# A two-layer trunk on one core: the feed-forward network in units of 1024 columns, half of its k-tiles as seven block products

## The chip, the core and the metric

The kernel runs on one core of a Trainium2 chip. The time is device time of one execution in microseconds (us), as a median of several. In the core, TensorE (PE) multiplies; its weight loads are counted apart (PEld). VectorE (DVE) and ScalarE (ACT) compute on tiles of 128 partitions, GpSimd (POOL) does little here, and SyncE (SP) issues the DMA transfers. Matmuls write to PSUM, everything else lives in SBUF.

## What is computed

Two layers over 256 tokens of width 2048, in fp32. Each has an input projection to 7168 columns, a gated and an attention branch, an output projection, and a feed-forward network (FFN) of width 5632:

```python
for l in range(DEPTH):                      # 2
    z = rms_norm(x, mix_norm[l]) @ w_in[l]  # 2048 x 7168
    mixed = ...                             # gated half and dilated attention, each normed
    x = x + mixed @ w_out[l]
    h = rms_norm(x, ffn_norm[l])
    x = x + (silu(h @ w_gate[l]) * (h @ w_up[l])) @ w_down[l]
```

w_gate and w_up are 2048 x 5632, w_down 5632 x 2048.

## The kernel before

Every fp32 product is made of three matmuls: an operand is split into a high and a low part (fp32r), and high x high, high x low and low x high are added in PSUM (L787 to L789). A matmul takes 128 rows of k, 128 tokens and 512 columns. A `Block` is 256 tokens x 512 columns: for each k-tile of 128 rows six matmuls, three for each token tile, into two PSUM banks `Z0`, `Z1`. A k-tile's six matmuls take 1.36 us.

Weights stream through a ring. `dma_to` (L685) fetches two k-tiles (`KC = 2`, 512 KB) into `raw`, five buffers. `split_to` has ACT copy them to `wh` (rounded to fp32r) and DVE compute `wl = raw - wh`, both 128x1024; four buffers each, three pairs ahead of the matmuls. All ACT, DVE and POOL instructions go through one helper, so they carry line L86.

An FFN layer is eleven times a gate block and an up block (16 k-tiles each) and then four down blocks of 44 k-tiles. After a gate block ACT makes `s = silu(Z * r2)`; after an up block DVE multiplies `s` by `Z * r2`, PE transposes it (8 transposes into `hTp`, L246), ACT and DVE split the result into `hTh` and `hTl`. A down block is added to the residual `xs` at its end. This side work is written as generators ("jobs"); rough clocks of the queues decide at build time, after every k-tile, which step is issued next. The order on each engine is then fixed, and each engine goes through its list in order.

Of the kernel before, what the change touches and what calls it, by code (L numbers as in the profile page):

```python
# [103 lines left out]
class Lease:  # L104
    """A count of buffers; each comes back at a time of the queue clocks."""
# [17 lines left out]
class Block:  # L123
    """One [256 tokens, 512 columns] output block: a list of k-tiles streamed through PSUM."""

    def __init__(self, src, kts, operand, done):
        self.src = src
        self.kts = kts
        self.operand = operand
        self.done = done  # L130
# [3 lines left out]
def trunk_kernel(ctx: ExitStack, tc: tile.TileContext, aps: dict):  # L134
# [6 lines left out]
    t2_lease = Lease(q, 5)  # L141
# [137 lines left out]
    for l, L in enumerate(layers):  # L279
# [26 lines left out]
    # ------------------------------------------------------------ layer consts  # L306
    def layer_consts(L):
# [30 lines left out]
    # ---------------------------------------------------------------- mixer  # L338
    def qk_done(L, pair, first):
        """Two kinds (k and q of group 0, or q of groups 1 and 2) of two heads each: RMS norm per  # L340
        head, rotary, transposition to [head dim, token]."""
        def job(Z):
# [11 lines left out]
            yield from t2_lease.take(4)  # L354
# [538 lines left out]
```

## Time and profile before

| | |
|---|---|
| median of 3 runs | 2343.61 us (2343.33 to 2343.93) |
| the profiled execution: span | 2342.1 us |
| PE busy | 2334.6 us (100%) |
| DVE busy | 1299.6 us (55%) |
| ACT busy | 1120.8 us (48%) |
| DMA moved | 440.23 MB, mean 188 GB/s |

The profile is of one execution; its span goes from the first to the last instruction, and the median of the runs is 1.5 us above it. Matmul rows overlap each other: a row's length is not the time from one to the next.

### The profile page before, as it was taken

How to read it: one execution, taken by the hardware profiler on the slowest of the kernel's cores; microseconds unless marked ns; L12 is line 12 of the kernel's file. 1: busy time of each engine (PE TensorE's matmuls, PEld its weight loads, DVE VectorE, ACT ScalarE, POOL GpSimd, SP SyncE). 2: the span in 40 equal slices, each digit the busy share in tenths (PEclk: the TensorE clock that was granted, in tenths of full speed). 3: DMA queues.
4: the chain of work that ended last, by engine and by line, in shares of the span. 5: the costliest groups of instructions: out<-in, count | busy, mean ns of one | idle time of the engine just before them, and what ended most of it. 6: DMA issues, size and time to landing. Idle time of an engine off the chain costs nothing.

```text
span 2342.1 us, 27917 instructions
## 1 busy us (share of the span) xinstructions
PE 2334.6 (100%) x10633; PEld 1937.0 (83%) x10633; DVE 1299.6 (55%) x1587; ACT 1120.8 (48%) x1548; POOL 43.3 (2%) x36
## 2 busy tenths in 40 slices
PE   9999999999999999999999999999999999999999
PEld 7888888888888888888888888888888888888887
DVE  6676676645445445444465667765454454454443
ACT  6556565544444444444455565655444444443333
POOL 0000000000000000000000000000000000000000
PEclk9999999999999999999999999999999999999999
DMA  8655555666565566556665555556666565556664
GB/s 301 208 173 169 173 160 180 189 190 190 187 193 192 185 193 190 189 190 192 192 195 194 175 164 178 162 180 183 195 187 190 189 188 190 190 193 194 201 201 135
DMA packets 122822, 440.23 MB, mean 188 GB/s; under 512 B 14272, under 2 KB 14784, under 8 KB 122432
## 3 DMA queue, kind: packets, MB, share of 16 engines
q1 hardware_dynamic: 122688, 438.45, 59.1%
q8 instruction: 83, 1.36, 0.2%
q14 instruction: 51, 0.42, 0.0%
HBM read 436.30 MB, written 2.10 MB: 187 GB/s over the span
## 4 chain that ended last, share of the span: by engine, by line
PE 99%; DMA 0%; DVE 0%; SPq 0%; ACT 0%; issue 0%
PE Z L789 32%; PE Z L787 32%; PE Z L788 32%; PE sc L448 1%; PE hTp L246 1%; PE qkp L246 1%; PE o L480 0%; PE xTp L246 0%; PE gt L543 0%; DMA raw<-in_w_in 0%; PE pT L471 0%; PE aTp L246 0%; PE bTp L246 0%; DVE xs L86 0%; DVE wl L86 0%; ACT wh L86 0%
## 5 line engine op out<-in xcount | busy, mean ns | idle before, releaser
L86 DVE TENSOR_TENSOR wl<-raw,wh 128x1024 fp32r<-128x1024 f32 (+1 forms) x817 | 999.3, 1224 | 992.3 <-ACT wh L86 991.7
L86 ACT ACTIVATE wh<-raw 128x1024 fp32r<-128x1024 f32 (+1 forms) x817 | 864.1, 1059 | 1082.8 <-PE Z L789 1040.6
L787 PE MATMUL Z<-wh,xTh 128*128 128x512 f32 x2304 | 911.0, 395 | 1.5 <-ACT wh L86 1.5
L789 PE MATMUL Z<-wh,xTl 128*128 128x512 f32 x2304 | 898.2, 390 | 0.0
L788 PE MATMUL Z<-wl,xTh 128*128 128x512 f32 x2304 | 897.1, 389 | 0.8 <-DVE wl L86 0.8
L789 PEld LDWEIGHTS Z<-wh,xTl 128*128 128x128 f32 x2304 | 432.4, 188 | 91.6 <-DVE xTl L86 0.2
L787 PEld LDWEIGHTS Z<-wh,xTh 128*128 128x128 f32 x2304 | 432.9, 188 | 89.5 <-ACT wh L86 2.8
L788 PEld LDWEIGHTS Z<-wl,xTh 128*128 128x128 f32 x2304 | 433.1, 188 | 87.9 <-DVE wl L86 1.5
L787 PE MATMUL Z<-wh,hTh 128*128 128x512 f32 x704 | 274.4, 390 | 0.0
L789 PE MATMUL Z<-wh,hTl 128*128 128x512 f32 x704 | 274.0, 389 | 0.0
L788 PE MATMUL Z<-wl,hTh 128*128 128x512 f32 x704 | 273.9, 389 | 0.0
L789 PEld LDWEIGHTS Z<-wh,hTl 128*128 128x128 f32 x704 | 132.1, 188 | 27.6
L787 PEld LDWEIGHTS Z<-wh,hTh 128*128 128x128 f32 x704 | 132.2, 188 | 27.3
L788 PEld LDWEIGHTS Z<-wl,hTh 128*128 128x128 f32 x704 | 132.2, 188 | 27.2
L86 ACT ACTIVATE p<-s,m 128x384 f32<-128x384 f32 (+1 forms) x32 | 24.9, 777 | 56.3 <-DVE m L86 56.2
L787 PE MATMUL Z<-wh,bTh 128*128 128x512 f32 x128 | 50.7, 396 | 0.0
L787 PE MATMUL Z<-wh,aTh 128*128 128x512 f32 x128 | 50.0, 391 | 0.0
L789 PE MATMUL Z<-wh,bTl 128*128 128x512 f32 x128 | 49.9, 390 | 0.0
L789 PE MATMUL Z<-wh,aTl 128*128 128x512 f32 x128 | 49.9, 389 | 0.0
L788 PE MATMUL Z<-wl,bTh 128*128 128x512 f32 x128 | 49.8, 389 | 0.0
L788 PE MATMUL Z<-wl,aTh 128*128 128x512 f32 x128 | 49.8, 389 | 0.0
L86 ACT ACTIVATE junk<-Z,r 128x128 bf16<-128x128 f32 x128 | 46.5, 363 | 5.5 <-POOL r L86 2.4
(98 smaller groups left out, 1014.4 us busy)
## 6 DMA issues: line engine op xcount, KB each, us to landing
raw<-in_w_in SPq DMA_DIRECT2D x223, 512.0 KB, 3.5
raw<-in_w_gate SPq DMA_DIRECT2D x176, 512.0 KB, 3.5
raw<-in_w_up SPq DMA_DIRECT2D x176, 512.0 KB, 3.5
raw<-in_w_down SPq DMA_DIRECT2D x176, 512.0 KB, 3.4
raw<-in_w_out SPq DMA_DIRECT2D x64, 512.0 KB, 3.5
xstage<-in_xT SPq DMA_DIRECT2D x8, 256.0 KB, 7.2
xs<-in_x SPq DMA_DIRECT2D x2, 1024.0 KB, 9.2
out<-xs SPq DMA_DIRECT2D x8, 256.0 KB, 2.2
```

What stands on the lines that cost most here:

```text
L86: return f(**kw)
L246: nc.tensor.transpose(out=tp[:, i, t * P:(t + 1) * P], in_=src_of(t)[:, (c0 + i) * P:(c0 + i + 1) * P], identity=ident)
L448: nc.tensor.matmul(out=sc[:, g, :n], lhsT=L.kv[pair, g][:, h, t * P:(t + 1) * P], rhs=kT[:, h, :n], start=True, stop=True)
L787: nc.tensor.matmul(out=Z[t], lhsT=hi, rhs=wh[:, k, :], start=n == 0, stop=False)
L788: nc.tensor.matmul(out=Z[t], lhsT=hi, rhs=wl[:, k, :], start=False, stop=False)
L789: nc.tensor.matmul(out=Z[t], lhsT=lo, rhs=wh[:, k, :], start=False, stop=n == len(b.kts) - 1)
```

## The change

In the FFN a unit is now 256 tokens x 1024 columns: the gate and the up block of one column tile, or two neighbouring down blocks. Of its k-tiles, eight (columns 0 and 1 of the operand, four k-tiles each) are treated as a 2 x 2 block product: the operand's blocks are (token tile) x (k half), the weights' (k half) x (column half). Seven products take the place of eight (Winograd's form of Strassen's method). The other k-tiles stay plain, in items of four k-tiles and one column half (24 matmuls).

The seven products r1, r5, r6, r2, r7, r3, r4 need seven weights: three blocks as they are, and e = b22 - b12, b12 - b11, e + b11 and b21 less that, four DVE sums of 128x2048. Each is then split as before, now in 128x2048 pieces (names p1 to p7 in the code, in the same order). They also need seven operands (`FORMS`), made by `make_forms` with four DVE sums and seven splits of 128x512. Sums of products are formed in four PSUM banks C1, CX, CY, CZ: after r1 ACT copies C1 to CX, after r5 CZ to `s5`, after r6 CX to CY, after r7 CX to `s3`; DVE then adds s3 to CZ and s5 to CY. Then come the plain items: gate 2, up 2, gate 3, up 3 (gate columns in C1 and CX, up columns in CY and CZ). Up 2 starts only when both sums are made.

The down product is taken in three chunks of k (`CHUNKS`): after four gate/up units two down units over their 16 k-tiles, the same again, and after the last three two down units whose treated pair is only two k-tiles wide (products of 6 matmuls). After each down unit DVE adds the four banks to `xs`.

Buffers are now one pool `gen` of 22 slots of 8 KB, for operands, raw weights, splits and tables alike; weights may hold five raw slots and six split slots in the FFN. The input and output projections stay blocks of 512 columns, with transfers of four k-tiles (1 MB). The four PSUM banks are leased one by one.

On PE 384 of 9792 main matmuls go.

DVE in the middle of a gate/up unit of layer 0. `wl` is a low half, `s` the gated product, `hTl` or `hF` low parts of h. Before:

```order
L86 TENSOR_TENSOR wl_5730<-raw_5661,wh_5729 128x1024
L86 TENSOR_TENSOR wl_5748<-raw_5679,wh_5747 128x1024
L86 TENSOR_TENSOR wl_5768<-raw_5697,wh_5767 128x1024
L86 SCALAR_TENSOR_TENSOR s_5635<-Z0_5615,r20_3967,s_5635 128x512
L86 SCALAR_TENSOR_TENSOR s_5636<-Z1_5616,r20_3967,s_5636 128x512
L86 TENSOR_TENSOR wl_5788<-raw_5715,wh_5787 128x1024
L86 TENSOR_TENSOR wl_5818<-raw_5733,wh_5817 128x1024
L86 TENSOR_TENSOR hTl_5806<-hTp_5807,hTh_5805 128x512
L86 TENSOR_TENSOR wl_5838<-raw_5751,wh_5837 128x1024
L86 TENSOR_TENSOR hTl_5806<-hTp_5812,hTh_5805 128x512
L86 TENSOR_TENSOR wl_5858<-raw_5771,wh_5857 128x1024
L86 TENSOR_TENSOR wl_5876<-raw_5791,wh_5875 128x1024
```

After, in the unit that also makes the forms of a chunk:

```order
L90 TENSOR_TENSOR wl_4110<-raw_3967,wh_4109 128x2048
L90 TENSOR_TENSOR raw_3909<-raw_3967,raw_3909 128x2048
L90 TENSOR_TENSOR wl_4133<-e_3998,wh_4132 128x2048
L90 TENSOR_TENSOR wl_4153<-raw_3949,wh_4152 128x2048
L90 TENSOR_TENSOR wl_4181<-raw_3909,wh_4180 128x2048
L90 TENSOR_TENSOR wl_4201<-raw_4060,wh_4200 128x2048
L90 TENSOR_TENSOR CZ_4116<-CZ_4116,s3_4130 128x512
L90 TENSOR_TENSOR wl_4221<-raw_4114,wh_4220 128x2048
L90 TENSOR_TENSOR hF_4232<-xg_3891,hF_4232 128x512
L90 TENSOR_TENSOR wl_4244<-raw_4136,wh_4243 128x2048
L90 TENSOR_TENSOR CY_4150<-CY_4150,s5_4129 128x512
L90 TENSOR_TENSOR hF_4232<-xg_3891,hF_4232 128x512
```

Before there is one kind of piece, 128x1024, with small work between; now 128x2048 pieces, a sum of weights (`raw` or `e` as the output) between them, and the sums into CZ and CY behind several of them.

ACT around the silu of a gate block. Before:

```order
L86 ACTIVATE wh_5579<-raw_5507 128x1024
L86 ACTIVATE wh_5597<-raw_5527 128x1024
L86 ACTIVATE wh_5617<-raw_5547 128x1024
L86 ACTIVATE s_5635<-Z0_5451,r20_3967 128x512
L86 ACTIVATE s_5636<-Z1_5452,r20_3967 128x512
L86 ACTIVATE wh_5639<-raw_5565 128x1024
L86 ACTIVATE wh_5657<-raw_5583 128x1024
L86 ACTIVATE wh_5675<-raw_5601 128x1024
L86 ACTIVATE wh_5693<-raw_5621 128x1024
```

After, from the end of the unit that makes the forms to the first copy of the next unit:

```order
L90 ACTIVATE wh_4309<-raw_4184 128x2048
L90 ACTIVATE wh_4338<-raw_4204 128x2048
L90 ACTIVATE hF_4233<-xg_3891 128x512
L90 ACTIVATE wh_4370<-raw_4184 128x2048
L90 ACTIVATE hF_4233<-xg_3891 128x512
L90 ACTIVATE hF_4234<-xg_3891 128x512 x2
L90 ACTIVATE fF_3286<-xg_3891 128x512
L90 ACTIVATE s_4384<-C1_4093,r20_3748 128x512
L90 ACTIVATE s_4386<-CX_4107,r20_3748 128x512
L90 ACTIVATE CX_4403<-C1_4390 128x512
```

The silu of C1 stood directly behind weight halves; it now stands behind the high parts of five forms.

DVE where the FFN of layer 0 begins: the low parts of the last four columns of the normed x (`xTl`, now `fT`). Before:

```order
L86 TENSOR_TENSOR wl_3892<-raw_3819,wh_3891 128x1024
L86 TENSOR_TENSOR wl_3924<-raw_3837,wh_3923 128x1024
L86 SCALAR_TENSOR_TENSOR xTl_3912<-xTp_3913,ffng_88,xTh_3911 128x256 x2
L86 TENSOR_TENSOR wl_3946<-raw_3855,wh_3945 128x1024
L86 SCALAR_TENSOR_TENSOR xTl_3912<-xTp_3918,ffng_88,xTh_3911 128x256 x2
L86 TENSOR_REDUCE rs_3968<-fss0_95 128x2
L86 TENSOR_SCALAR rsq_3970<-rs_3968 128x2
L86 TENSOR_TENSOR wl_3974<-raw_3875,wh_3973 128x1024
L86 TENSOR_TENSOR wl_3992<-raw_3895,wh_3991 128x1024
L86 TENSOR_TENSOR wl_4010<-raw_3927,wh_4009 128x1024
L86 TENSOR_TENSOR wl_4028<-raw_3949,wh_4027 128x1024
```

After, inside the first gate/up unit:

```order
L90 TENSOR_TENSOR wl_3661<-raw_3570,wh_3660 128x2048
L90 TENSOR_TENSOR CY_3584<-CY_3584,s5_3563 128x512
L90 SCALAR_TENSOR_TENSOR fT_3686<-fTp_3687,ffng_81,fT_3686 128x256 x2
L90 TENSOR_TENSOR wl_3709<-raw_3590,wh_3708 128x2048
L90 TENSOR_TENSOR e_3712<-raw_3646,raw_3627 128x2048
L90 TENSOR_TENSOR raw_3627<-raw_3627,raw_3608 128x2048
L90 TENSOR_TENSOR wl_3740<-raw_3608,wh_3739 128x2048
L90 TENSOR_TENSOR raw_3608<-e_3712,raw_3608 128x2048
L90 SCALAR_TENSOR_TENSOR fT_3686<-fTp_3692,ffng_81,fT_3686 128x256 x2
L90 TENSOR_REDUCE rs_3749<-fss0_88 128x2
L90 TENSOR_SCALAR rsq_3751<-rs_3749 128x2
```

Between the two pairs of low parts stood one piece of 128x1024; now two splits and three sums of 128x2048 stand there, among them those of the next unit.

The core of the diff; lines that are only "..." mark what is left out:

```diff
@@ -30,15 +30,19 @@
 NQ = len(DIL)
 EPS = 1e-6
 BIG = 1e30
-KC = 2
-
-RAW_BUFS = 5
-W_BUFS = 4
-SPLIT_AHEAD = 3
-DMA_AHEAD = SPLIT_AHEAD + RAW_BUFS - 1
-GEN_BUFS = 30
-
-MM_NS = 214
+KC = 4
+HK = 2
+S_GU = 4
+FORMS = ("11", "22", "S1", "S3", "S2", "12", "S4")
+
+SLOTS = 22
+PLAIN_RAW, PLAIN_RING = 3, 4
+UNIT_RAW, UNIT_RING = 5, 6
+CHUNKS = ((4, 4), (4, 4), (3, 2))
+
...
-    t2_lease = Lease(q, 5)
+    t2_lease = Lease(q, 2)
+    rot_lease = Lease(q, 1)
     sd_lease = Lease(q, 2)
     sc_lease = Lease(q, 1)
     unit_lease = Lease(q, UNITS)
...
-    raw_p = ctx.enter_context(tc.tile_pool(name="raw_p", bufs=RAW_BUFS))
-    w_p = ctx.enter_context(tc.tile_pool(name="w_p", bufs=W_BUFS))
-    tmp = ctx.enter_context(tc.tile_pool(name="tmp", bufs=5))
+    gen = ctx.enter_context(tc.tile_pool(name="gen", bufs=SLOTS))
...
+    def make_forms(F, xg):
+
+        def quarter(t, h):
+            return xg[:, h, :F.s, t * P:(t + 1) * P]
+        a11, a12, a21, a22 = quarter(0, 0), quarter(0, 1), quarter(1, 0), quarter(1, 1)
+
+        def split(f, src):
+            hi, lo = F.at(f)
+            act.activation(out=hi, in_=src, func=ACTF.Copy)
+            dve.tensor_tensor(out=lo, in0=src, in1=hi.bitcast(F32), op=ALU.subtract)
+            F.ready.add(f)
+        split("11", a11)
+        yield
+        split("22", a22)
+        yield
+        dve.tensor_tensor(out=a22, in0=a21, in1=a22, op=ALU.add)
+        dve.tensor_tensor(out=a21, in0=a11, in1=a21, op=ALU.subtract)
+        yield
+        split("S1", a22)
+        yield
+        dve.tensor_tensor(out=a11, in0=a22, in1=a11, op=ALU.subtract)
+        split("S3", a21)
+        yield
+        split("12", a12)
+        yield
+        split("S2", a11)
+        yield
+        dve.tensor_tensor(out=a12, in0=a12, in1=a11, op=ALU.subtract)
+        split("S4", a12)
+
+
...
+    class Chunk:
+
+
+        def __init__(self, L, j0, n, s):
+            self.L, self.j0, self.n, self.s = L, j0, n, s
+            self.table, self.F, self.xg = {}, None, None
+
+        def put_h(self, j, src_of):
...
+                self.F = F
+                yield from make_forms(F, self.xg)
+
...
+    def gu_bank(L, j, chunk):
+
+        s = {}
+
+        def done(n, t, bank):
+            if n == 0:
+                yield lambda: hasattr(L, "r2")
+                yield from t2_lease.take(1)
+                s[t] = t2("s")
+                act.activation(out=s[t], in_=bank, func=ACTF.Silu, scale=L.r2[:, t:t + 1])
+                mm_lease.give()
+                return
+            yield lambda: t in s
+            dve.scalar_tensor_tensor(
+                out=s[t], in0=bank, scalar=L.r2[:, t:t + 1], in1=s[t], op0=ALU.mult, op1=ALU.mult)
             mm_lease.give()
-            L.s[j] = s
-        return job
...
+    def dma_one(r):
+        n = sum(src.shape[1] for src in r.srcs)
+        r.tile = slot([P, n, W], F32, "raw")
+        k = 0
+        for src in r.srcs:
+            nc.sync.dma_start(out=r.tile[:, k:k + src.shape[1], :], in_=src)
+            k += src.shape[1]
+        live[0] += 1
...
+    def w_sum(out, in0, in1, op):
+        saved, q.chain = q.chain, q.pe
+        dve.tensor_tensor(out=out, in0=in0, in1=in1, op=op)
+        q.chain = saved
+
+    def mm3(out, x, wh, wl, start, stop):
+        hi, lo = x
+        for n, (a, b) in enumerate(((hi, wh), (hi, wl), (lo, wh))):
+            nc.tensor.matmul(
+                out=out, lhsT=a, rhs=b, start=start and n == 0, stop=stop and n == 2,
+                skip_group_check=True)
...
+    def unit(s, quarter, plains, form, done):
+
+
+
+        bank = {}
+        b11, b12, b22, b21 = (Raw([quarter(*kn)], UNIT_RAW) for kn in ((0, 0), (0, 1), (1, 1), (1, 0)))
+        raws.extend((b11, b12, b22, b21))
+        U = {}
+
+        def new_bank(name):
+            drain(lambda: mm_lease.free)
+            mm_lease.free.pop(0)
+            bank[name] = mm_p.tile([P, W], F32, tag="mm", name="C" + name)
+
+        def copy(out, in_):
+            saved, q.chain = q.chain, q.pe
+            act.activation(out=out, in_=in_, func=ACTF.Copy)
+            q.chain = saved
+
+        def early():
+            x11, x12, x22 = need(b11), need(b12), need(b22)
+            U["e"] = slot([P, s, W], F32, "e")
+            live[0] += 1
+            w_sum(U["e"], x22, x12, ALU.subtract)
+            w_sum(x12, x12, x11, ALU.subtract)
+
+        def p1(it, parts=1):
+            it.w = split_w(b11.tile)
+            w_sum(b11.tile, U["e"], b11.tile, ALU.add)
+
+        def p5(it, parts=1):
+            it.w = split_w(b12.tile)
+            live[0] -= 1
+
+        def p6(it, parts=1):
+            it.w = split_w(b11.tile)
+
+        def p2(it, parts=1):
+            it.w = split_w(need(b21))
+            w_sum(b11.tile, b21.tile, b11.tile, ALU.subtract)
+            live[0] -= 1
+
+        def p7(it, parts=1):
+            it.w = split_w(U["e"])
+            live[0] -= 1
+
+        def p3(it, parts=1):
+            it.w = split_w(b22.tile)
+            live[0] -= 1
+
+        def p4(it, parts=1):
+            it.w = split_w(b11.tile)
+            live[0] -= 1
+
+        def product(it, f, name, start):
+            wh, wl = it.w
+            for k in range(s):
+                x = form(f, k)
+                mm3(bank[name], x, wh[:, k, :], wl[:, k, :], start and k == 0, k == s - 1)
+                q.pe += 3 * MM_NS
+                run_jobs()
+
+        def r1(it):
+            new_bank("1")
+            product(it, "11", "1", True)
+            new_bank("X")
+            copy(bank["X"], bank["1"])
+
+        def r5(it):
+            new_bank("Z")
+            product(it, "S1", "Z", True)
+            U["s5"], U["s3"] = (tmp.tile([P, W], F32, tag="u", name=n) for n in ("s5", "s3"))
+            copy(U["s5"], bank["Z"])
+
+        def r6(it):
+            product(it, "S2", "X", False)
+            new_bank("Y")
+            copy(bank["Y"], bank["X"])
+
+        def r2(it):
+            product(it, "12", "1", False)
+
+        def r7(it):
+            product(it, "S3", "X", False)
+            copy(U["s3"], bank["X"])
+
+            def sums():
+                dve.tensor_tensor(out=bank["Z"], in0=bank["Z"], in1=U["s3"], op=ALU.add)
+                yield lambda: "p3" in U
+                yield from pause(0)
+                dve.tensor_tensor(out=bank["Y"], in0=bank["Y"], in1=U["s5"], op=ALU.add)
+                U["summed"] = True
+            add(sums(), FFN_LIMIT)
+
+        def r3(it):
+            product(it, "S4", "Y", False)
+            U["p3"] = True
+
+        def r4(it):
+            product(it, "22", "X", False)
+
+        for p, r in ((p1, r1), (p5, r5), (p6, r6), (p2, r2), (p7, r7), (p3, r3), (p4, r4)):
+            items.append(Item(1 if s <= 2 else 2, UNIT_RING, p, r))
+        items[-7].early = early
+
+        names = {(0, 0): "1", (1, 0): "Y", (0, 1): "X", (1, 1): "Z"}
+        for i, (n, srcs, ops) in enumerate(plains):
+            r = Raw(srcs, UNIT_RAW)
+            raws.append(r)
+
+            def prep(it, parts=1, r=r):
+                it.w = split_w(need(r))
+                live[0] -= 1
+
+            def run(it, i=i, n=n, ops=ops):
+                wh, wl = it.w
+                for t in range(NT):
+                    if n == 1:
+                        drain(lambda: "summed" in U)
+                    for k, op in enumerate(ops):
+                        mm3(bank[names[n, t]], op(t), wh[:, k, :], wl[:, k, :], False, k == len(ops) - 1)
+                        q.pe += 3 * MM_NS
+                        run_jobs()
+                    if i >= len(plains) - 2:
+                        add(done(n, t, bank[names[n, t]]), FFN_LIMIT)
+            items.append(Item(2, UNIT_RING, prep, run))
+
     for l, L in enumerate(layers):
         L.xss = const.tile([P, NT, 4], F32, name=f"xss{l}")
...
+    def prep_next(parts=1):
+        it = items[n_prep[0]]
+        it.prep(it, parts)
+        n_prep[0] += 1
+        held[0] += it.slots
+        if n_prep[0] < len(items) and items[n_prep[0]].early:
+            items[n_prep[0]].early()
+
+    def prep_more():
+        while n_prep[0] < len(items) and held[0] + items[n_prep[0]].slots <= items[n_prep[0]].cap:
+            prep_next()
+            dma_more()
...
```

## Rows read from the trace of the kernel before

**Rows 1.** Page: busy us and share of PE; the chain that ended last.
```profile
PE 2334.6 (100%) x10633; PEld 1937.0 (83%) x10633; DVE 1299.6 (55%) x1587; ACT 1120.8 (48%) x1548; POOL 43.3 (2%) x36
PE 99%; DMA 0%; DVE 0%; SPq 0%; ACT 0%; issue 0%
```

**Rows 2.** Windows: busy us of PE, PEld, DVE, ACT, POOL; clock; DMA; GB/s.
```profile
0.00:5.50 5.50, 4.02 (x9) 1.19 (x9) 1.18 (x4) 2.04 (x3) 0.70 (x6) 1.00 0.57 168
...
500.00:1100.00 600.00, 600.00 (x2697) 497.79 (x2696) 297.00 (x269) 256.18 (x272) 0.00 (x0) 1.00 0.61 190
```

**Rows 3.** Groups by form: instruction, count | busy us, mean ns | idle before.
```profile
L86 DVE TENSOR_TENSOR wl<-raw,wh 128x1024 fp32r<-128x1024 f32 x815 | 997.9, 1225 | 991.8 <-ACT wh L86 991.3
...
L787 PE MATMUL Z<-wh,xTh 128*128 128x512 f32 x2304 | 911.0, 395 | 1.5 <-ACT wh L86 1.5
...
L86 ACT ACTIVATE wh<-raw 128x1024 fp32r<-128x1024 f32 x815 | 862.8, 1060 | 1080.0 <-PE Z L789 1040.6 <-issue 25.4 <-DMA raw<-in_w_in 6.2
```

**Rows 4.** Timeline of ACT in the FFN: start us, duration us, instruction.
```profile
701.13 1.06 ACT L86 ACTIVATE wh<-raw 128x1024 fp32r<-128x1024 f32 x1 [1.66 <-PE Z L789]
...
709.29 1.06 ACT L86 ACTIVATE wh<-raw 128x1024 fp32r<-128x1024 f32 x1 [1.66 <-PE Z L789]
```

**Rows 5.** Chain that ended last, around 714 us: start us, duration us, what.
```profile
714.70 0.87 PE hTp L246 x8
715.57 0.23 PE Z L787
```

**Rows 6.** Groups by form: the small operations and the 512-column halves.
```profile
L86 DVE SCALAR_TENSOR_TENSOR s<-Z,r,s 128x512 f32<-128x512 f32 x44 | 30.8, 742 | 0.0
...
L86 DVE TENSOR_TENSOR hTl<-hTp,hTh 128x512 fp32r<-128x512 f32 x44 | 30.0, 683 | 0.0
...
L86 ACT ACTIVATE s<-Z,r 128x512 f32<-128x512 f32 x44 | 27.5, 675 | 0.0
...
L86 ACT ACTIVATE hTh<-hTp 128x512 fp32r<-128x512 f32 x44 | 25.5, 579 | 0.0
...
L86 DVE SCALAR_TENSOR_TENSOR xTl<-xTp,ffng,xTh 128x256 fp32r<-128x256 f32 x32 | 15.4, 481 | 9.7 <-ACT xTh L86 9.7
...
L86 DVE TENSOR_TENSOR wl<-raw,wh 128x512 fp32r<-128x512 f32 x2 | 1.4, 692 | 0.5 <-ACT wh L86 0.3
...
L86 ACT ACTIVATE wh<-raw 128x512 fp32r<-128x512 f32 x2 | 1.3, 632 | 2.8 <-DMA raw<-in_w_in 2.8
```

**Rows 7.** Timelines of DVE (702, 1382 us) and ACT (1395 us).
```profile
702.23 1.23 DVE L86 TENSOR_TENSOR wl<-raw,wh 128x1024 fp32r<-128x1024 f32 x1 [1.49 <-ACT wh L86]
...
1382.02 1.23 DVE L86 TENSOR_TENSOR wl<-raw,wh 128x1024 fp32r<-128x1024 f32 x1 [0.96 <-ACT wh L86]
1383.17 0.48 DVE L86 SCALAR_TENSOR_TENSOR bTl<-bTp,bog,bTh 128x256 fp32r<-128x256 f32 x1
...
1395.32 1.99 ACT L86 ACTIVATE wh<-raw 128x1024 fp32r<-128x1024 f32 x2
```

**Rows 8.** Page: GB/s in 40 slices of the span; landing time of a transfer.
```profile
GB/s 301 208 173 169 173 160 180 189 190 190 187 193 192 185 193 190 189 190 192 192 195 194 175 164 178 162 180 183 195 187 190 189 188 190 190 193 194 201 201 135
...
raw<-in_w_gate SPq DMA_DIRECT2D x176, 512.0 KB, 3.5
```

**Rows 9.** Timeline of PE at the start.
```profile
1.25 4.02 PE L761 MATMUL warm<-junk 128*128 128x512 bf16 x9 [1.25 <-DVE junk L756]
5.64 0.72 PE L787 MATMUL Z<-wh,xTh 128*128 128x512 f32 x1 [0.37 <-ACT wh L86]
...
6.70 0.39 PE L789 MATMUL Z<-wh,xTl 128*128 128x512 f32 x1
6.93 0.39 PE L787 MATMUL Z<-wh,xTh 128*128 128x512 f32 x1
...
10.28 0.50 PE L787 MATMUL Z<-wh,xTh 128*128 128x512 f32 x1 [1.09 <-ACT wh L86]
11.54 0.50 PE L788 MATMUL Z<-wl,xTh 128*128 128x512 f32 x1 [0.76 <-DVE wl L86]
```

More of the change, by code (lines that the diff above doesn't have):

```diff
@@ L120, in give, with __init__ @@
         self.free += [self.q.chain] * n
[L123 to L130, printed above, removed]
+class Raw:
+    def __init__(self, srcs, cap):
+        self.srcs, self.cap, self.tile = srcs, cap, None
+class Item:
+    def __init__(self, slots, cap, prep, run):
+        self.slots, self.cap, self.prep, self.run = slots, cap, prep, run
+        self.early = None
 @with_exitstack
@@ L353, in job @@
             yield lambda: L.tab_ready
-            yield from t2_lease.take(4)
+            yield from rot_lease.take()
+            rot = slot([P, 4, W], F32, "rot")
             f2 = stat("qf2", [P, NT, HH])
@@ L393, in job @@
             yield from sd_lease.take(2)
-            dst = slot([P, HH, SEQ], F32, "qkT")
+            if pair not in L.kvt:
+                L.kvt[pair] = slot([P, 2, HH, SEQ], F32, "qkT")
+            dst = L.kvt[pair][:, 0 if first else 1]
             tps = [transpose_pair(lambda t: ro[t], 2 * pr, "qkp") for pr in range(2)]
-            t2_lease.give(2)
+            rot_lease.give()
             yield
@@ L498, in job @@
                 vg.append(a)
-            mm_lease.give()
+            mm_lease.give(2)
             yield
@@ new lines, in down_bank, with done @@
+    def down_bank(L, pair, chunk, last):
+        N = layers[L.l + 1] if L.l + 1 < DEPTH else None
+        left = {0: NT, 1: NT}
+        def done(n, t, bank):
+            j = 2 * pair + n
+            cols = slice(j * W, (j + 1) * W)
+            dve.tensor_tensor(out=xs[t][:, cols], in0=bank, in1=xs[t][:, cols], op=ALU.add)
+            mm_lease.give()
+            if last and N is None:
+                nc.sync.dma_start(out=aps["out"][t * P:(t + 1) * P, cols], in_=xs[t][:, cols])
+            left[n] -= 1
+            if not last or N is None or left[n]:
@@ new lines, in split_w @@
+    def split_w(src, parts=1):
+        n = src.shape[1]
+        if 2 * n <= 4:
+            both = slot([P, 2, n, W], F32R, "w")
+            wh, wl = both[:, 0], both[:, 1]
+        else:
+            wh, wl = slot([P, n, W], F32R, "wh"), slot([P, n, W], F32R, "wl")
+        saved, q.chain = q.chain, q.pe
+        for k in range(parts):
+            sl = slice(k * n // parts, (k + 1) * n // parts)
+            act.activation(out=wh[:, sl, :], in_=src[:, sl, :], func=ACTF.Copy)
+            dve.tensor_tensor(
+                out=wl[:, sl, :], in0=src[:, sl, :], in1=wh[:, sl, :].bitcast(F32), op=ALU.subtract)
+        q.chain = saved
+        return wh, wl
@@ L707, in first_xT @@
+    def prep_next(parts=1):
[9 more added lines that the diff above has]
+            dma_more()
     def first_xT(L):
         nc.sync.dma_start(out=mixg, in_=aps["mix_norm"])
-        stage = [slot([P, 4, SEQ], F32, "xstage") for _ in range(4)]
+        stages = [slot([P, 2, 4, SEQ], F32, "xstage") for _ in range(2)]
+        stage = [st[:, h] for st in stages for h in range(2)]
+        parts = [(r, k, 1 if n == 0 and k < HK else HK)
+                 for n in range(PLAIN_RAW) for r in (raws[n],)
+                 for k in ((0, 1, 2) if n == 0 else (0, 2))]
+        take = [2] + [1] * 7
```

355 lines of the change are left out of this document (213 added, 142 removed).

## The prediction

> **What bounds the kernel now.** The page's head comes first: TensorE (PE) is busy for 2334.6 of 2342.1 us and the chain that ended last is PE to 99% [rows 1]. The windows then show whether one stage is different: in 500 to 1100 us, inside layer 0's FFN, PE is busy for 600.00 of 600 us while VectorE (DVE) has 297.00 and ScalarE (ACT) 256.18 [rows 2]. So a main matmul taken away there is worth its full pitch, and DVE and ACT have 300 and 340 us of room in 600. The groups show what feeds PE: ACT makes the high half of each pair of k-tiles in 1060 ns, DVE the low half in 1225 ns [rows 3]. The pitch of a matmul is read from ACT, which starts once per 12 matmuls: 701.13 to 709.29 is three such steps, 8.16 us, so 36 matmuls take 0.2267 us each [rows 4]. (The 390 ns of a row in [rows 3] overlap; they are no pitch.) The eight transposes of an h tile put 0.87 us between two matmuls [rows 5].
>
> **What is removed.** A product of seven for eight saves one eighth of the treated matmuls. A gate/up unit before had 2 x 16 k-tiles x 6 = 192 matmuls; now it has 7 x 12 + 4 x 24 = 180. Eleven such units a layer and four wide down units save 12 each, two narrow down units 6 each: 11 x 12 + 4 x 12 + 2 x 6 = 192 a layer, 384 in all, 384 x 0.2267 = **-87.05 us**. The built program's order has just that many fewer, so that the change saves no matmuls is no rival. It is collected in full only if PE never waits.
>
> **What DVE and ACT gain.** The new operations are larger than any in the trace. DVE's difference takes 692 ns at 512 columns and 1225 at 1024 [rows 3, 6], a slope of 533 per 512, so 2048 is estimated at 2.29 us; ACT's copy goes 632, 1060, so 1.92 us. Back to back an operation begins about 0.08 us before the one ahead is over (1382.02 + 1.23 against 1383.17), and two ACT copies take 1.99 us [rows 7], so I use steps of 2.21 and 1.79 us; the dearer end is 2.29 and 0.1 for further waits, the DVE rival below. A cheaper one has no row. ACT's copy from PSUM to PSUM and DVE's sum in PSUM aren't in the trace either: ACT's nearest rows are 579 (PSUM to SBUF) and 675 ns (silu), DVE's 683 and 742 [rows 6]; I take 0.6 and 0.69, and the dearer end, 0.1 each on a chain, is 34 x 0.1 = 3 us. A gate/up unit asks DVE for 11 differences and 4 sums of weights, 15 x 2.21 = 33.2 us, two sums in PSUM and two low halves of h (683 ns) and two gated products (742 ns) [rows 6], some 4.2 us: 37.4 us. PE needs 180 x 0.2267 + 0.87 = 41.7 us. DVE is at 90%, not over; ACT has 11 x 1.79 + some 5 us = 25. On throughput PE stays the bound. What remains is order: DVE and ACT work strictly through their lists, and a list at 90% answers late to anything that stands behind 2.2 us pieces. The sum is therefore one of PE's waits, unit by unit, each walked from r1's start.
>
> **r7 in each unit.** The weights of r7's product are e = b22 - b12, made early, but its low half stands on DVE behind low p2 and the sum b21 - b11. ACT's high p2 stands behind the copy of C1, which can start only when r1 is done: 2.72 + 0.16 (the drain), copy 0.6 (579 ns [rows 6]) to 3.5, high p2 to 5.3, low p2 to 7.6, sum to 9.8, low p7 to 12.0. PE reaches r7's second matmul at 4 x 2.72 + 0.23 = 11.1: **1.08 us** where no transposes stand ahead of r7, 0.23 where they do. Five units a layer of the first kind (first of each chunk, second down unit of the first two), the rest of the second.
>
> **CY's sum.** PE needs CY + s5 before the first up matmul, at 7 x 2.72 + 0.87 + 0.23 + 5.44 = 25.6. DVE has it behind low p7 (12.0), low p3, p4, gate2, CZ's sum, low up2 and gate3, 12.0 + 5 x 2.21 + 0.69 + 0.69 = 24.4: in time. In the two units a layer that also make forms, and in the first down units, two small parts (0.69) stand there too and some 0.2 of handover: 26.0, **0.4 late**. In the last gate/up unit one more makes it 1.0.
>
> **After the forms.** When the second h column of a chunk is there, DVE and ACT make seven operands (11 x 0.69 us on DVE). One is put into a slot that the last plain item (up3) holds until its last low matmul, and the next unit's first matmul needs C1's bank, whose silu stands on ACT behind these splits. From PE's end: ACT 0.58, DVE 3 x 0.62, ACT 0.58, silu 0.68 and the handovers of 0.04 each [rows 6, 7] are 3.9 at least; if DVE, which has 37.4 + 7.6 = 45 us of work in that unit, is late, 5.75. I take 4.6, nearer the lower end, since the earlier waits let DVE run ahead. Two a layer.
>
> **First unit of a layer.** Its third plain item reads columns 3 of the normed x. Their last two low parts (481 ns each) stand on DVE behind five pieces of the next unit, 5 x 2.21 us. PE gets there at 34.4 us; DVE at 38.9 when nothing else is late, 2.1 later when e waits for its transfer: 4.6 to 6.7, taken 5.6.
>
> **Last chunk.** Its down units have products of 6 matmuls (1.36 us) while DVE's sum CY + s5 comes behind 11 pieces of 1.15 us and three low halves of 2.21 us: at 20.9 us, where PE needs it at 7 x 1.36 + 0.87 + 5.44 = 15.8: 5.2. Ahead of it the same effect as after the forms costs 2.1, as r1 is short. In the second down unit of layer 0 ACT's two PSUM copies also stand behind squares and splits of the next layer's x, 1.5 + 2.8 + 5.2 = 9.5. Layer 1 has no next layer: 2.5.
>
> **Sum.** First chunk: 1.08 + 5.6 + 0.23 + 0.63 + 4.6 + 0.23 + 0.65 + 1.08 = 14.1. Second: the same without 5.6 = 8.5. Third: 1.08 + 0.23 + 1.23 + 2.1 + 5.2 + 9.5 = 19.3. Layer 0 41.9, layer 1 34.9, together **+76.8 us**. The last product's tail is 0.7 shorter. The input and output projections keep their matmuls; their transfers are 1 MB instead of 512 KB, and a transfer of 512 KB lands after 3.5 us, the slices after the first moved 135 to 208 GB/s and the first 301 [rows 8]; a unit now asks for 8.4 MB in 42 us, 200 GB/s, so I put them at 0 (up to +5 if the first 1 MB is late). 2342.1 - 87.05 - 0.7 + 76.8 = 2331.1, and the median lies 1.5 us above the profiled span: **2333 us**, its own range 2310 to 2352 (low ends of the waits with DVE running ahead, high ends of each term). 0.2%, 4.7 us, is about what a measurement here tells from no change.
>
> **Rivals.**
> The cover holds (0.2): waits of one unit let DVE catch up so far that the CY and forms waits shrink to their floors (3.9, 0) and the first unit's is gone; only some 20 to 50 us of wait remain, **2277 to 2307**. For it: DVE idle for 303 of 600 us before. Against: the three-step chains have floors that no lead removes.
>
> DVE decides (0.16): steps of 2.29 plus 0.1 for an instruction with three or four waits, 15 x 2.39 + 4.5 = 40.4 us, leaves no slack; each unit's CY sum is late by another 0.7, 34 x 0.7 = 24 us: **2357**, slower. It decides from a step of 2.3 us on. Against: two-wait differences start 0.04 us after ACT in the trace [rows 7].
>
> PE's clock (0.2): the first nine matmuls, after 1.25 us without work, took 4.02 us, 0.45 each, and from 6.70 on the step is 0.23 [rows 9], although the granted clock reads 1.00 in that stretch [rows 2]; gaps of 1.09 and 0.76 us later did no such harm. Twice the step is what the 1.2 GHz level would give against 2.4. The new waits of 4 to 9.5 us (some ten) are longer than any gap in this trace. If each is followed by as many matmuls at that step as at the start, nine, it loses 9 x 0.22 = 2 us: 10 x 2 = 20, **2353**, slower. It decides from some five such gaps on.
> The Trainium skill ("TensorE: Matmul & The Clock Gate", "The HAM clock gate") says this of idle stretches: the array goes back to half rate and has to be busy again to be released. The start of this trace agrees with 0.45 against 0.2267; no row here shows it after a gap.
>
> **How the numbers follow.** The forecast has 0.44: faster 0.30, same 0.09, slower 0.05. The cover rival is all faster (0.20). The clock rival: 0.15 slower, 0.05 same. DVE: slower. Faster 0.50, same 0.14, slower 0.36. With the cover rival to 2288 and both slow rivals at once, 2333 + 20 + 24 = 2377 cut to 2372, about 2 in 10 is left out: 2288 to 2372.
>
> **What would show it.** 384 matmuls fewer; DVE near 80% (some 1880 us), ACT near 59%; PE's waits put down to DVE wl ahead of r7 (about 1 us, ten times), to ACT's silu after the forms (four of 4 to 6 us), to DVE's fT (two of 5), to CY's sum in the last chunk. If PE has under 50 us of gaps the cover rival is right; if matmuls after a gap step by 0.45, the clock rival; if CY's sum is waited for in most units, DVE's. Wrong altogether if transfers end most waits, or the projections' windows lose PE time.

## The result and the profile after

The changed kernel takes 2386.04 us (2385.62 to 2387.71), 1.8% more than before: the ratio is 1.018, with an interval of 1.0166 to 1.0195. The profiled execution's span is 2383.6 us, against 2342.1 before. The page and the clock of the core:

```profile
span 2383.6 us, 25937 instructions
PE 2289.1 (96%) x10249; PEld 1878.5 (79%) x10249; DVE 1830.2 (77%) x1721; ACT 1325.7 (56%) x1590; POOL 52.5 (2%) x36
core 0: 2383.6 us, clock 0.984
```

PE has 384 matmuls fewer than in [rows 1], as counted. It is now without work for 94.5 of 2383.6 us, where it was 7.5 before. But it is also busy for 2289.1 us, and 2334.6 - 87.05 would be 2247.6: 41.5 us more than its remaining matmuls need. Two things ate the gain, and the clock line, 0.984 in place of 1.00, names the second.

The first are PE's waits (in order: who waits, for whom, us in total, times, longest):

```profile
PE C L840 <- ACT s L90: 26.2, 6, 5.8
PE CY L840 <- DVE CY L90: 19.6, 14, 5.1
PE C L840 <- DVE xs L90: 17.2, 2, 8.6
PE C L840 <- DVE fT L90: 12.2, 2, 6.1
PE CX L840 <- DVE wl L90: 7.8, 10, 0.8
PE CX L840 <- ACT s L90: 2.5, 1, 2.5
...
PE CX L840 <- ACT CY L90: 1.1, 1, 1.1
```

Together 86.6 us in the FFN, almost exactly the 87.05 that the removed matmuls were worth. Not one of them is for a DMA.

The second: the longest wait of layer 0 and what PE does behind it. Timeline of PE (start, duration, instruction, idle before it and its releaser), then windows with the columns of [rows 2], around the same place:

```profile
453.12 0.76 PE L840 MATMUL C<-wh,fF 128*128 128x512 f32 x1 [8.63 <-DVE xs L90]
453.68 0.63 PE L840 MATMUL C<-wl,fF 128*128 128x512 f32 x1
454.10 1.05 PE L840 MATMUL C<-wh,fF 128*128 128x512 f32 x2
...
459.69 0.39 PE L840 MATMUL CZ<-wl,fF 128*128 128x512 f32 x1
459.92 0.62 PE L840 MATMUL CZ<-wh,fF 128*128 128x512 f32 x2
```

```profile
453.12:459.12 6.00, 6.00 (x14) 4.74 (x15) 1.82 (x3) 0.51 (x2) 0.00 (x0) 0.50 0.00 0
459.12:465.12 6.00, 6.00 (x27) 4.89 (x27) 4.07 (x2) 4.99 (x6) 0.00 (x0) 0.99 0.44 150
```

After 8.63 us without work the granted clock is 0.50, the 1.2 GHz level, and matmuls start 0.42 us apart (453.68 to 454.10); from 459.2 on it is 1.00 and they start 0.23 apart. In equal windows there are 14 matmuls and 27. Eleven such stretches stand in the two FFNs, each behind a wait of 4.7 to 8.6 us. From the end of each wait to where the clock is whole again they hold 52 us; half of that, 26 us, is lost. The Trainium skill ("TensorE: Matmul & The Clock Gate", "The HAM clock gate") has the array back at half rate after an idle stretch, until it has been busy again; here the trace agrees, with 0.42 against 0.23.

### The profile page after: what moved, and what is told of

It is laid out like the page before. It is cut to its first block, busy times and chain, and to the rows that moved or that the text cites. A ratio compares the mean times of both kernels' runs of the same rounds, so it can differ in the third digit from the quotient of the medians.

```text
span 2383.6 us, 25937 instructions
## 1 busy us (share of the span) xinstructions
PE 2289.1 (96%) x10249; PEld 1878.5 (79%) x10249; DVE 1830.2 (77%) x1721; ACT 1325.7 (56%) x1590; POOL 52.5 (2%) x36
## 5 line engine op out<-in xcount | busy, mean ns | idle before, releaser
L90 DVE TENSOR_TENSOR wl<-raw,wh 128x2048 fp32r<-128x2048 f32 x316 | 718.1, 2285 | 191.6 <-ACT wh L90 189.3
L90 ACT ACTIVATE wh<-raw 128x2048 fp32r<-128x2048 f32 x316 | 597.6, 1912 | 208.3 <-PE CX L840 76.5
L840 PE MATMUL Z<-w,xT 128*128 128x512 f32 x2688 | 640.6, 395 | 2.8 <-ACT w L90 1.5
L840 PEld LDWEIGHTS Z<-w,xT 128*128 128x128 f32 x2688 | 498.8, 188 | 106.9 <-ACT w L90 2.4
L90 DVE TENSOR_TENSOR w<-raw,w 128x1024 fp32r<-128x1024 f32 (+1 forms) x313 | 377.2, 1216 | 219.9 <-ACT w L90 215.0
L90 ACT ACTIVATE w<-raw 128x1024 fp32r<-128x1024 f32 (+1 forms) x313 | 316.2, 1049 | 47.8 <-DVE raw L90 29.5
L840 PE MATMUL CX<-wh,fF 128*128 128x512 f32 x528 | 174.8, 391 | 0.0
L840 PE MATMUL C<-wh,fF 128*128 128x512 f32 x352 | 130.0, 427 | 40.2 <-ACT s L90 23.0
L90 DVE TENSOR_TENSOR raw<-raw 128x2048 f32<-128x2048 f32 (+1 forms) x68 | 147.1, 2163 | 1.2
L840 PE MATMUL CX<-wh,fT 128*128 128x512 f32 x352 | 117.6, 394 | 0.0
```

What stands on the lines that cost most here:

```text
L90: return f(**kw)
L840: nc.tensor.matmul(out=out, lhsT=a, rhs=b, start=start and n == 0, stop=stop and n == 2, skip_group_check=True)
```

## Experiments

All twelve start from the changed kernel. The kernel before, run beside each group of them, took 2344.1 to 2345.7 us (medians), so differences between groups are good to some 2 us; the ratios are to the runs beside. Theory C was: the waits come from the order of work on DVE and ACT, and each long one costs a second time through the clock. The rivals: the clock does nothing (W), and DVE's load decides, whatever the order (D).

**e1_busy: only the clock.** PE gets work in its longest waits, nothing else moves.

```diff
+    def busy(n):
...
+        t = sc_p.tile([P, 2 * W], F32, tag="sc", name="busy")
+        flat = masks.rearrange("p g k -> p (g k)")
+        for _ in range(n):
+            nc.tensor.matmul(
+                out=t[:, :W], lhsT=flat[:, :P], rhs=flat[:, :W], start=True, stop=True)
...
         def r1(it):
+            busy(warm[0])
             new_bank("1")
```

> Only PE's idle time in the eleven longest waits is filled: extra bf16 matmuls of 512 columns (36 ahead of the first unit's r1, 22 ahead of the third k-tile of its gate3 item, 22 ahead of r1 of the two units after the forms, 18 ahead of the first up item of the last chunk's down units; 2 layers, 219 in all), into a bank that is free there, short enough to end before the wait does. The order on DVE, ACT and SP is unchanged. Theory C (clock): the waits stay, the stretches at half the granted clock after them (some 52 us of active matmuls, losing 26 us) are gone: 2386 - 26 = 2360 us (2354 to 2366). Rival W (only the waits count; slow matmuls after a wait are starved, not clocked down): 2386 us within 4.

Measured: 2365.52 us (ratio to before 1.0085, 1.007 to 1.01), 20.5 us less than the changed kernel, clock 0.999. The first unit begins at full speed, behind the same wait (both of its ends are 0.94 us later):

```profile
core 0: 2363.7 us, clock 0.999
452.62 0.59 PE L881 MATMUL busy<-masks 128*128 128x512 bf16 x2
454.06 0.47 PE L840 MATMUL C<-wh,fF 128*128 128x512 f32 x1 [0.85 <-DVE xs L90]
454.36 0.39 PE L840 MATMUL C<-wl,fF 128*128 128x512 f32 x1
454.59 0.63 PE L840 MATMUL C<-wh,fF 128*128 128x512 f32 x2
```

The extra matmuls are 258, as the code and the trace have it (102 a layer and three times 18), and not the 219 written down; with them the kernel is 20 us faster. W is out: what follows a long wait is the clock. Of the 26 us that the steps give, 20 came back. Read from start to start, 1.6 us at half clock are left in the FFNs (behind a wait of 2.54 us), steps a little over 0.23 add 2.6, and the waits with the extra matmuls in them are as long as they were (92.7 us, 92.5 in the changed kernel); the blocks ahead of the first FFN, which the edit doesn't touch, take 1.6 more. A PE that is slow after a wait gives DVE time: in the first unit the wait for r7's low half, 0.46 us in the changed kernel, is 0.83.

**e2_silu: one wait removed, and what took its place.** The planner gets the gated product's two tiles back after their transposes.

```diff
             yield from raw_T(src_of, self.xg[:, i], None, "hTp")
+            free()
...
-            t2_lease.give(2)
```

> The two tiles of the gated product come back to the planner after their transposes and not after the forms of the chunk, so that the silu of the next C1 is issued on ACT ahead of the last form splits. Theory C: the four waits of 5.75 us for ACT's silu go (23 us) with the half clock behind them (22 us active, 11 lost): 2386 - 34 = 2352 us. Rival W (no clock effect): 2363. Rival D (DVE has 45 us of work in these units, so the wait only moves to another of its products): 2375 to 2386.

Measured: 2423.64 us (1.0332, 1.0314 to 1.0349): 38 us worse, beyond every expectation. The waits of 5.75 us for the silu of C1 are gone from PE's list, but those for CY have grown:

```profile
PE CY L841 <- DVE CY L90: 64.5, 18, 11.4
PE C L841 <- DVE xs L90: 17.2, 2, 8.6
```

PE's longest wait of layer 0, and DVE's timeline ahead of it:

```profile
630.05 0.77 PE L841 MATMUL CY<-wh,fT 128*128 128x512 f32 x1 [11.32 <-DVE CY L90]
618.70 0.68 DVE L90 TENSOR_TENSOR hT<-hTp,hT 128x512 fp32r<-128x512 f32 x1
619.30 0.68 DVE L90 TENSOR_TENSOR xg<-xg 128x512 f32<-128x512 f32 x1
620.67 0.69 DVE L90 TENSOR_TENSOR fF<-xg,fF 128x512 fp32r<-128x512 f32 x1 [0.69 <-ACT fF L90]
622.48 2.29 DVE L90 TENSOR_TENSOR wl<-raw,wh 128x2048 fp32r<-128x2048 f32 x1 [1.11 <-ACT wh L90]
624.68 2.28 DVE L90 TENSOR_TENSOR e<-raw 128x2048 f32<-128x2048 f32 x1
627.00 2.29 DVE L90 TENSOR_TENSOR raw<-raw 128x2048 f32<-128x2048 f32 x1
629.21 0.69 DVE L90 TENSOR_TENSOR CY<-CY,s 128x512 f32<-128x512 f32 x1
```

PE needs CY's sum at 618.7 (it starts at 630.05 after 11.32 us). The rest of the forms now stands in this unit, with a wait for ACT in it (0.69 us) and one behind it (1.11), and the planner put CY behind that, behind the unit's last weight piece and behind two sums of the next unit. The work of DVE is that of the changed kernel (1832.5 us against 1830.2; the forms had to be made somewhere); its place is what costs. So the wait moved, as rival D said, but for a reason of order.

**e3_wout and e4_order: two other waits.** Side work of the output projection without regard to the backlog; gate items ahead of up items.

```diff
-                        add(done(st["Z"]))
+                        add(done(st["Z"]), limit)
...
+                None, FFN_LIMIT)
```

```diff
+        plains = [p for p in plains if p[0] == 0] + [p for p in plains if p[0] == 1]
+        ends = [max(i for i, p in enumerate(plains) if p[0] == n) for n in range(2)]
...
-                    if i >= len(plains) - 2:
+                    if i in ends:
```

> The side work after an output-projection block is issued without regard to the backlog of ACT and DVE (its limit goes from 4000 to 30000 ns), so that the sums into xs and the normed columns stand ahead of more weight pieces. Theory C: the two waits for fT (12.2 us) go, the two for xs (17.2 us) at least halve, and with them some 20 us at half clock (10 lost): 2347 to 2356 us. W: 2357 to 2366. Rival D: the weight pieces that are pushed back are waited for instead: 2380 or more.

> In each unit the gate items stand ahead of the up items (gate2, gate3, up2, up3 in place of gate2, up2, gate3, up3), so CY + s5 is needed 5.4 us later. Theory C: the 14 waits for CY (19.6 us) go with the half clock after three of them (5 us lost), while gate3 of the first unit comes 5.4 us earlier and waits that much longer for fT, twice: 2386 - 25 + 11 = 2372 us. W: 2377. Rival D (DVE is late with everything): the wait moves to the weights of the up items, 2384 to 2392.

Measured: 2370.30 us (1.0106, 1.0091 to 1.0121) and 2363.19 us (1.0077, 1.0062 to 1.0092), 16 and 23 us less. In e3_wout the fT wait is gone and the xs wait falls from 17.2 to 5.9, with 2.5 new at CZ, but CY's grows from 19.6 to 24.9. It fell short of my 30 to 39. In e4_order CY's waits are gone; it did better than expected, because the longer wait for fT that I had added didn't come (12.3): DVE, asked in another order, was earlier too. Its silu waits grew from 26.2 to 31.4, which I had not expected.

**e5_all and e6_wout_order: together.**

> The three edits of the second to fourth run together (gated product's tiles back early, output-projection side work without regard to the backlog, gate items ahead of up items). Without any wait and at full clock the changed kernel would take about 2265 us (2386 less some 94 of waits and 27 of half clock). Theory (waits by order, and the clock behind each long one): left are ten waits for r7's low half (8.4), the rest of the xs waits (8.4), some 6 in the last chunk, and of the CY waits that the second run moved to 11.4 us, four, the part beyond the 5.4 us by which the new order puts the need later (24), with 10 for the clock behind these: 2322 us (2300 to 2335). Rival D (DVE's load): the sum of the waits does not fall below that of the third and fourth run, 2345 or more.

> Third and fourth edit together, the gated product's tiles come back as in the changed kernel. Theory: the silu waits stay (31 us in the fourth run), xs 8.4, r7 8.4, 3 others, and the clock behind four to six waits 12: 2265 + 63 = 2328 us; the edits are additive, 2386 - 16 - 23 = 2347, only if the fT wait of the fourth run (12.3) stays.

Measured: all three edits 2342.39 us (0.9993, 0.9983 to 1.0003), the two without e2's 2336.45 us (0.9964, 0.9951 to 0.9977). CY's four waits stand in e5_all just as expected:

```profile
PE CY L841 <- DVE CY L90: 23.7, 4, 6.0
```

But the time is 20 us above the 2322 that I had written down. Some 7 of them are half clock (17 us, read from the steps, where I had 10), some 7 are waits (54 us, where I had 47), and the base of 2265 was too low: it leaves out all 94 us in which PE is without work, and the kernel before has 7.5 of these too. e6_wout_order is beyond additive (2347), and 8 above my 2328: its silu waits stay (31.7), fT's is gone. Both lie below D's bound of 2345, e5_all by less than 3 us; the waits say it more clearly, 54 us in the FFN where e3_wout and e4_order have over 70.

**e7_pool and e8_all_pool: less work on DVE.** Two of the four weight sums go to GpSimd.

```diff
-            w_sum(U["e"], x22, x12, ALU.subtract)
-            w_sum(x12, x12, x11, ALU.subtract)
+            nc.gpsimd.tensor_tensor(out=U["e"], in0=x22, in1=x12, op=ALU.subtract)
+            nc.gpsimd.tensor_tensor(out=x12, in0=x12, in1=x11, op=ALU.subtract)
```

> The changed kernel with two of the four weight sums of a unit (b22 - b12 and b12 - b11) on GpSimd in place of DVE, 4.4 of DVE's 37 to 45 us per unit. Theory (order): chains of three to five pieces get shorter where a sum stood in them: fT 2 x 4.4, CY in the last chunk 2 x 2, the silu waits from 5.75 to their floor of 4, xs unchanged, r7 unchanged: 2386 - 20 - 5 (clock) = 2361 us (2352 to 2372). Rival D (DVE's load decides): most waits go, 2335 or less. Rival P (GpSimd takes long for 128x2048 or holds DVE up): 2386 or more, with DVE's 128x2048 pieces above 2.29 us.

> All three edits of order and the two sums on GpSimd. Theory: as the run with the three edits, less some 10 for the shorter chains: 2312 us. Rival P: above the run with the three edits.

Measured: 2462.75 us (1.0506, 1.049 to 1.0521) and 2366.78 us (1.0098, 1.0083 to 1.0113): both worse than their bases. DVE's differences in the changed kernel, then groups by form of e7_pool and two of its GpSimd sums with the DVE differences beside them:

```profile
L90 DVE TENSOR_TENSOR wl<-raw,wh 128x2048 fp32r<-128x2048 f32 x316 | 718.1, 2285 | 191.6 <-ACT wh L90 189.3
...
L90 DVE TENSOR_TENSOR wl<-raw,wh 128x2048 fp32r<-128x2048 f32 x316 | 879.8, 2800 | 176.4 <-ACT wh L90 174.0 <-DMA raw<-in_w_down 2.3
...
L899 POOL TENSOR_TENSOR raw<-raw 128x2048 f32<-128x2048 f32 x30 | 187.1, 6236 | 2.4
L898 POOL TENSOR_TENSOR e<-raw 128x2048 f32<-128x2048 f32 x30 | 162.4, 5414 | 1067.9 <-DVE wl L90 303.4 <-DMA raw<-in_w_down 287.6 <-PE CX L840 244.8
...
477.63 4.61 POOL L898 TENSOR_TENSOR e<-raw 128x2048 f32<-128x2048 f32 x1 [41.46 <-DVE wl L90]
482.31 6.42 POOL L899 TENSOR_TENSOR raw<-raw 128x2048 f32<-128x2048 f32 x1
...
477.99 12.89 DVE L90 TENSOR_TENSOR wl<-raw,wh 128x2048 fp32r<-128x2048 f32 x2
```

GpSimd takes 5.4 and 6.2 us for what DVE does in 2.29, and DVE's own differences lengthen from 2285 to 2800 ns on average: 316 x 0.515 = 163 us more, against the 137 of the sixty wide sums. It is the 66 of them that run beside a GpSimd sum that lengthen, to 4742 ns on average; the other 250 take 2288. DVE is left busier than it was, for 1886.7 us against 1830.2. So these two runs don't test D, only rival P, which is right. The Trainium skill ("GPSIMD Engine Reference", "3.1 Elementwise — side-by-side cycle accounting") has 4497 ns for an add of this length; here it took 5414 and 6236 on average with DVE at work. The Trainium skill ("GPSIMD Engine Reference", "8. Key points") also says that the engine shares its SBUF interfaces with VectorE and contends with DVE instructions that read two inputs there; the 4742 against 2288 ns agree.

**e10_p7, e9_all_cy_p7, e11_cy_p7, e12_all_cy: the r7 wait, and CY's place.** Two edits: b21 - b11 behind low p7 (p7), and CY + s5 issued at the start of r4 by hand instead of by the planner (cy).

```diff
         def p2(it, parts=1):
             it.w = split_w(need(b21))
-            w_sum(b11.tile, b21.tile, b11.tile, ALU.subtract)
...
         def p7(it, parts=1):
             it.w = split_w(U["e"])
...
+            w_sum(b11.tile, b21.tile, b11.tile, ALU.subtract)
```

```diff
-                yield lambda: "p3" in U
-                yield from pause(0)
-                dve.tensor_tensor(out=bank["Y"], in0=bank["Y"], in1=U["s5"], op=ALU.add)
-                U["summed"] = True
+                yield
...
         def r4(it):
+            w_sum(bank["Y"], bank["Y"], U["s5"], ALU.add)
+            U["summed"] = True
```

> The changed kernel with one edit: b21 - b11 is issued behind low p7 instead of ahead of it. It prices the term for r7: its waits in the trace (10 of up to 0.84 us, 7.8 us, and some short ones) go, nothing else moves: 2386 - 9 = 2377 us (2374 to 2380). Rival (DVE's load): the gain is given back at CY's sum, 2386.

> The run with three edits, and two more edits of order on DVE: CY + s5 is issued at the start of r4 instead of by the planner, and b21 - b11 stands behind low p7 instead of ahead of it. Theory: the four CY waits of 5.9 us (23.7) go with the half clock behind them (27 us of clock, 8 lost, in the four), the waits for r7's low half (11.8) go: 2342 - 43 = 2299 us (2290 to 2315). Rival: DVE, late by then, answers the next thing late instead (the up items' weights, or the silu), 2325 or more.

> The same two edits on the run with the third and fourth edit, where the silu of C1 still stands behind the forms. Theory: the waits for r7's low half (8.7) go, the silu waits (31.7) stay with their clock: 2336 - 9 = 2327 us (2322 to 2332). Rival: CY's sum, now ahead of PE's need at a fixed place, holds DVE up until r3 is done, 2336 or more.

> The run with five edits less the one on r7 (b21 - b11 stands ahead of low p7 again). In the changed kernel alone that edit gave nothing: the wait of 0.84 us moved from r7 to the next product. If that holds here too, the whole gain from 2342 to 2319 us is that of issuing CY + s5 at the start of r4: 2319 us (2315 to 2323). If the edit on r7 helps once the longer waits are gone: 2326 or more.

Measured, e10_p7 (the changed kernel with p7): 2385.08 us (1.0172, 1.0157 to 1.0187), no gain. Its waits say why, where the 7.8 at CX stood:

```profile
PE CY L840 <- DVE wl L90: 10.5, 14, 0.8
```

The same 0.8 us is waited for one product later, at r3, whose low half now stands behind the sum. The time is the rival's, but not for its reason: the waits at CY's sum are as they were (20.3 us, 19.6 in the changed kernel). Taking one piece out of the way of a chain helps only if the next product isn't late by as much.

The other three, each against before: e9_all_cy_p7 (e5_all with both) 2318.68 us, 0.9887 (0.9873 to 0.9902); e11_cy_p7 (e6_wout_order with both) 2340.02 us, 0.9979 (0.9969 to 0.9988); e12_all_cy (e5_all with cy alone) **2307.68 us, 0.9841 (0.9825 to 0.9858)**. So cy is worth 35 us on e5_all, and p7 costs 11 there, which I had not expected: neither e9_all_cy_p7 nor e12_all_cy came out as one of the cases written down for it. Some of the 11 show as new waits of e9_all_cy_p7, 4.8 us for the gated product and 1.8 for fT; the rest is open. e11_cy_p7 came out as its rival had it: on e6_wout_order, where PE doesn't wait for CY at all, the two edits gain nothing and cost 4 us; no run has cy alone there. e12_all_cy beats both kernels. Its busy times, waits and clock:

```profile
PE 2267.0 (98%) x10249; PEld 1866.5 (81%) x10249; DVE 1829.6 (79%) x1721; ACT 1326.3 (57%) x1590; POOL 52.6 (2%) x36
...
PE CX L841 <- DVE wl L90: 12.1, 14, 0.9
PE CX L841 <- ACT hF L90: 6.1, 2, 3.0
PE C L841 <- DVE xs L90: 5.9, 2, 3.0
PE CZ L841 <- DVE xs L90: 4.1, 2, 2.8
PE CY L841 <- ACT fF L90: 2.5, 2, 1.4
...
core 0: 2307.1 us, clock 0.996
```

DVE makes the same differences, sums and products as in the changed kernel, 1721 instructions and 1829.6 us against 1830.2; only their order differs, and 78 us went. That settles D: the load of DVE did not make the changed kernel slow.

## Why the prediction was wrong

It said 2333 us, faster, in a range of 2288 to 2372; the time lies above it. Step by step:

- **What is removed** held: 384 matmuls fewer. So did the durations estimated for shapes that no row of before had: DVE 128x2048 2285 ns (2.29 us), ACT 1912 ns (1.92), copies in PSUM 582 and 598 ns (0.6), sums in PSUM 692 and 691 ns (0.69). DVE is at 77% and ACT at 56%, where I had 80 and 59.
- **The waits that were walked** came where they were said, and close to their size: r7 0.84 (1.08, though the steps written down for it, 12.0 less 11.1, make 0.9), after the forms 5.75 each, the upper end (4.6 was taken), fT 6.1 (5.6), CY in the last chunk 5.06 (5.2), with small ones of 0.5 and 0.85 (0.4 and 1.0), ahead of it 1.6 (2.1), layer 0's last unit 1.1 + 2.5 + 4.7 = 8.3 (9.5), layer 1's none (2.5).
- **One wait was missed**: the first unit of each layer. I walked each unit from its r1's start, and so didn't ask what r1 waits for. All four PSUM banks are held by the last two output blocks, and their sums into xs stand on DVE behind a weight piece and the forms:

```profile
448.60 2.29 DVE L90 TENSOR_TENSOR wl<-raw,wh 128x2048 fp32r<-128x2048 f32 x1 [1.11 <-ACT wh L90]
450.81 0.48 DVE L90 SCALAR_TENSOR_TENSOR fT<-fTp,ffng,fT 128x256 fp32r<-128x256 f32 x1
451.83 0.48 DVE L90 SCALAR_TENSOR_TENSOR fT<-fTp,ffng,fT 128x256 fp32r<-128x256 f32 x1 [0.54 <-ACT fT L90]
452.23 1.40 DVE L90 SCALAR_TENSOR_TENSOR xs<-Z,rb,xs 128x512 f32<-128x512 f32 x2
```

  PE starts at 453.12, after 8.63 us; 17.2 for both layers. The term in the sum was 76.8, and PE's rows show 86.6: 69.4 without these two.
- **The step that failed**: the clock stood among the rivals, at 0.2, as if it were another outcome. It was a part of the same one: the sum itself held some ten waits of over 4 us, and [rows 9] showed 0.45 us a matmul after idle time. The price given there, 20 us, belonged into the sum. That e1_busy measured 20.5 is in part luck: the eleven stretches cost 25 us and not ten times 2, and not all of it came back when they were gone. With the 20 and the missed wait the working gives 2333 + 10 + 20 = 2363.
- **The rest** is in the trace too, when PE's rows are read from start to start. The half clock costs 25 us in the FFNs. The 36 waits cost 92.5 us where their rows show 86.6 of idle time, since a row of 0.39 us ends 0.16 us after the next one could have started. Steps at full clock with no idle time in front of them add 9 us (12.5 us over 0.2267 each in the two FFNs, where the kernel before has 3.2): waits too short for a row to show, two thirds of them at products into CX, where small terms for r7 had been forecast. That makes 10 + 6 + 25 + 9 = 50 of the 53 us between 2333 and 2386. The other 3 are a later first matmul (6.81 in place of 5.64), half clock in the first block (1.0), and a median 2.4 us above the span instead of 1.5.
- **The rivals**: the cover rival's idea that earlier waits shrink later ones is seen only once (0.46 in place of 0.83). The DVE rival fell with e12_all_cy, and its sign didn't come: CY's sum is waited for in 14 of 34 units. The clock rival's sign came (0.42), but its 2353 lies 33 us below the time, as the waits were under-sized beside it. The 1.00 of [rows 2] in the first 5.5 us was no evidence against it: the first record of the clock in that trace is at 6.14 us, and a stretch without a record reads as 1.00. Transfers end none of PE's waits, as said.

## What to carry to other kernels

When matmuls are saved by giving DVE and ACT more to do, a utilisation below 100% says little: walk the waits of one unit and of every seam between stages, the first instruction of the stage included, and add the clock's price to each long one rather than keep it as an alternative. An in-order queue that is filled far ahead turns a small urgent operation into a long wait; issue such an operation at a fixed place (here CY's sum, 35 us in the order that had waits for it) before thinking of moving work to another engine. And an edit that removes one wait has to be read from the trace: here one wait moved to the next product at the same length (e10_p7), and another came back elsewhere at twice the length (e2_silu, 5.75 us to 11.4).

## What the hardware showed that I had not expected

- The half clock also follows shorter waits, and their length alone doesn't say which. In the fourteen traces all 79 waits of PE of 4.0 us and more have it behind them. Of those between 2.0 and 3.6 us some have it and some have not. In e12_all_cy PE waits 2.98 us for xs and then has 7 matmuls in 3 us at a clock of 0.52; in e4_order a wait of 2.73 us has the same behind it. After a wait of 2.54 us in the changed kernel the clock stays at 1.00, but in e1_busy the same wait of 2.54 us has half clock behind it, and after 3.53 us in e11_cy_p7 it stays at 1.00. Windows of the five in this order, 3 us each behind the wait:

```profile
447.92:450.92 3.00, 3.00 (x7) 2.33 (x8) 3.00 (x3) 2.27 (x2) 0.00 (x0) 0.52 0.40 169
```

```profile
1118.46:1121.46 3.00, 3.00 (x7) 2.42 (x8) 1.39 (x2) 0.52 (x1) 0.00 (x0) 0.50 0.59 221
```

```profile
1169.83:1172.83 3.00, 3.00 (x13) 2.50 (x14) 1.21 (x1) 3.00 (x2) 0.00 (x0) 1.00 0.68 246
```

```profile
1160.27:1163.27 3.00, 3.00 (x8) 2.42 (x9) 1.23 (x1) 3.00 (x2) 0.00 (x0) 0.59 0.54 227
```

```profile
1103.56:1106.56 3.00, 3.00 (x13) 2.50 (x14) 1.39 (x2) 1.77 (x3) 0.00 (x0) 1.00 0.70 285
```

- Matmuls that compute nothing paid for themselves: 258 of them in the waits gave 20.5 us.
- A sum on GpSimd lengthens the DVE differences beside it: 4742 ns on average in e7_pool, where those with no such sum beside them take 2288.
